# Channel shuffle: tiles of 51 KB a partition in two load and two store buffers, for tiles of 38 KB in two and three

## The chip, the cores and the metric

The kernel runs on one core of a Trainium2 chip. Its time is the device time of one launch in microseconds (us); it was measured in three runs. One further execution was taken with the hardware profiler, and the profile and the trace below are of that one.

A core has several engines with queues of their own. Three matter here: VectorE (DVE in the profile), which does the copies; SyncE (SP), whose queue issues the loads; and ScalarE (ACT), whose queue issues the stores. The bytes themselves are moved by 16 transfer (DMA) engines. Data sits in the main memory of the chip (DRAM) and is worked on in a buffer memory of 128 partitions.

## The reference

The input `x` is 16 x 64 x 64 x 256 in float32, 67.1 MB, and `groups` is 8. Every run of 256 channels is read as 8 groups of 32 and written as 32 x 8, a small transpose:

```python
x = x.reshape(batch, h, w, groups, channels_per_group)
x = x.transpose(0, 1, 2, 4, 3)
x = x.reshape(batch, h, w, c)
```

Nothing is computed with the values. 67.1 MB are read and 67.1 MB are written.

## The kernel before

The 65,536 pixels of 256 channels are 1 KB each. A tile with `q` in the list of slots takes 128 x `q` pixels that follow one another, and each of the 128 partitions gets `q` of them, so `q` KB that are contiguous in DRAM. A transfer of a tile so has 128 rows of `q` KB. "A tile of 38" below is one with 38 KB a partition, 4.98 MB in all.

The list `_SLOTS` (line 12) gives the tiles in order. An entry is a slot: it has one load buffer and one store buffer, and its parts share these. The first slot has two parts, of 4 and 8 KB; then come a slot of 28, twelve of 38 and one of 16, which adds up to 512 KB a partition.

For each slot the loop (lines 45 to 63) takes the next buffer of `in_pool` and of `out_pool`, issues the loads of all its parts on SP's queue (line 55), and then for each part a copy on VectorE (line 57) and a store on ACT's queue (line 61). The copy reads the source in steps of 32 elements (group, then channel in the group) and writes a contiguous run. As built, its source is walked in three levels, rows x 32 x 8, and its destination as a single run of 256 x rows elements.

The order of each queue is that of the code (`manual_schedule`). What else orders the work are the buffers, which are used in turn:

- A load waits until the copy that reads its buffer is done. With two load buffers that is the copy two slots back.
- A copy waits for its load, and until the stores that read its store buffer have landed. With three store buffers those are the stores three slots back, with two those of two slots back.
- A store waits for its copy.

The buffers are as large as the biggest slot: 2 x 38 + 3 x 38 = 190 KB a partition.

Of the kernel before, what the change touches and what calls it, by code (L numbers as in the profile page):

```python
# [1 line left out]

# [4 lines left out]


F32 = mybir.dt.float32
P = 128  # L10

_SLOTS = [[4, 8], [28]] + [[38]] * 12 + [[16]]
_IN_BUFS = 2
_OUT_BUFS = 3


@with_exitstack
def kernel(
    ctx: ExitStack,
    tc: tile.TileContext,  # L20
    x: bass.AP,
    groups: bass.AP,
    out: bass.AP,
):
    nc = tc.nc
    b, h, w, c = x.shape
    G = int(groups)
    CPG = c // G
    assert G * CPG == c
    assert sum(map(sum, _SLOTS)) * P == b * h * w  # L30
    biggest = max(map(sum, _SLOTS))

    x_flat = x.rearrange("b h w c -> (b h w c)")
    out_flat = out.rearrange("b h w c -> (b h w c)")

    in_pool = ctx.enter_context(tc.tile_pool(name="in_pool", bufs=_IN_BUFS))
    out_pool = ctx.enter_context(tc.tile_pool(name="out_pool", bufs=_OUT_BUFS))

    def rows(flat, first, q):

        return flat[first * c : (first + P * q) * c].rearrange("(p f) -> p f", p=P)

    ctx.enter_context(tc.manual_schedule(engines=None))
    first = 0
    for parts in _SLOTS:
        in_tile = in_pool.tile([P, biggest * c], F32, name="in_tile")
        out_tile = out_pool.tile([P, biggest * c], F32, name="out_tile")
        at = 0
        pieces = []
        for q in parts:  # L50
            pieces.append((q, first, slice(at * c, (at + q) * c)))
            first += P * q
            at += q
        for q, start, cols in pieces:
            nc.sync.dma_start(out=in_tile[:, cols], in_=rows(x_flat, start, q))  # L55
        for q, start, cols in pieces:
            nc.vector.tensor_copy(  # L57
                out=out_tile[:, cols].rearrange("p (i j g) -> p i j g", j=CPG, g=G),
                in_=in_tile[:, cols].rearrange("p (i g j) -> p i j g", g=G, j=CPG),
            )  # L60
            nc.scalar.dma_start(
                out=rows(out_flat, start, q), in_=out_tile[:, cols]
            )


# [1 line left out]
_INS = ['x', 'groups']  # L67
_OUTS = [((16, 64, 64, 256), 'float32')]

_NUMBERS = {'groups': 8}  # L70


# [26 lines left out]
```

## Time and profile before

| | us |
|---|---|
| median of the three runs (316.06 to 316.10) | 316.07 |
| span of the profiled execution | 314.4 |
| VectorE busy, 16 copies | 119.0 |
| one copy of 38 KB (128 x 9728 elements), mean of 12 | 8.79 |
| load of 38 KB, median from issue to landing | 37.0 |
| store of 38 KB, median from issue to landing | 42.6 |
| start of the first copy | 4.06 |
| start of the last copy (the slot of 16) | 294.54 |

The span is the stretch from the first to the last instruction of the profiled execution. The profile says for each engine how long it was busy, and for each instruction what ended the idle time ahead of it. Transfers are listed with the time from the issuing instruction to the landing of the last byte; that time contains the wait behind earlier transfers of the same queue. Over the whole span the transfer engines moved 427 GB/s in the mean.

### The profile page before, as it was taken

The numbers are of one execution on the slowest core, as the hardware profiler recorded it, in microseconds if no ns is written. First come the engines' busy times: TensorE is split into PE (matmuls) and PEld (weight loads), VectorE is DVE, ScalarE is ACT, GpSimd is POOL, SyncE is SP. The second block draws the span as 40 slices with busy tenths as digits, with TensorE's granted clock in tenths as the row PEclk, the third lists the DMA queues.
The fourth block names the chain that finished last, engine by engine and source line by source line (L and its number), as shares of the span: only waits on it lengthen the run. The fifth ranks groups of instructions, "written<-read, shape, count | busy, mean of one in ns | idle before, by whom it ended". The sixth has DMA issues, their size and how long they took to land.

```text
span 314.4 us, 132 instructions
## 1 busy us (share of the span) xinstructions
DVE 119.0 (38%) x16; POOL 0.2 (0%) x4
## 2 busy tenths in 40 slices
DVE  2081907309109109019028028037046055065400
POOL 0000000000000000000000000000000000000000
DMA  7999999999999999999999999999999999999997
GB/s 317 405 441 416 435 416 483 401 465 406 450 421 446 426 436 436 401 470 396 475 396 475 396 470 401 470 401 470 401 450 421 446 426 436 436 417 450 429 421 321
DMA packets 4608, 134.22 MB, mean 427 GB/s; under 512 B 512, under 2 KB 512, under 8 KB 768
## 3 DMA queue, kind: packets, MB, share of 16 engines
q1 hardware_dynamic: 2304, 67.11, 49.8%
q10 hardware_dynamic: 2304, 67.11, 49.4%
HBM read 67.11 MB, written 67.11 MB: 427 GB/s over the span
## 4 chain that ended last, share of the span: by engine, by line
DMA 76%; DVE 19%; issue 0%; SPq 0%; DVEq 0%
DMA in_tile<-in_x_dram 76%; DVE out_tile L57 19%; SPq L55 0%; DVEq L57 0%
## 5 line engine op out<-in xcount | busy, mean ns | idle before, releaser
L57 DVE COPY out_tile<-in_tile 128x9728 f32<-128x9728 f32 (+4 forms) x16 | 119.0, 7440 | 179.4 <-DMA in_tile<-in_x_dram 179.4
L80 POOL MEMSET const-uint8-127<- 128x1 uint8 x1 | 0.1, 103 | 0.0
L80 POOL MEMSET const-bfloat16-1.0<- 128x1 bf16 x1 | 0.1, 102 | 0.0
L80 POOL MEMSET const-float32-1.0<- 128x1 f32 x1 | 0.1, 100 | 0.0
L80 POOL MEMSET const-float32-0.0<- 128x1 f32 x1 | 0.1, 99 | 0.2 <-issue 0.2
## 6 DMA issues: line engine op xcount, KB each, us to landing
in_tile<-in_x_dram SPq DMA_DIRECT2D x12, 4864.0 KB, 37.0
out_dram<-out_tile ACTq DMA_DIRECT2D x12, 4864.0 KB, 42.6
in_tile<-in_x_dram SPq DMA_DIRECT2D x1, 3584.0 KB, 14.7
out_dram<-out_tile ACTq DMA_DIRECT2D x1, 3584.0 KB, 30.9
in_tile<-in_x_dram SPq DMA_DIRECT2D x1, 2048.0 KB, 30.4
out_dram<-out_tile ACTq DMA_DIRECT2D x1, 2048.0 KB, 15.2
in_tile<-in_x_dram SPq DMA_DIRECT2D x1, 1024.0 KB, 5.4
out_dram<-out_tile ACTq DMA_DIRECT2D x1, 1024.0 KB, 25.0
```

What stands on the lines that cost most here:

```text
L57: nc.vector.tensor_copy(out=out_tile[:, cols].rearrange("p (i j g) -> p i j g", j=CPG, g=G), in_=in_tile[:, cols].rearrange("p (i g j) -> ...
L80: nc = _bacc.Bacc("TRN2", target_bir_lowering=False, num_devices=1)
```

## The change

```diff
-_SLOTS = [[4, 8], [28]] + [[38]] * 12 + [[16]]
+_SLOTS = [[4, 4], [28]] + [[51]] * 9 + [[17]]
 _IN_BUFS = 2
-_OUT_BUFS = 3
+_OUT_BUFS = 2
```

The sum over the slots stays 512 KB a partition. The first slot has parts of 4 and 4, the second stays, twelve tiles of 38 become nine of 51, and the last has 17 for 16. There are 13 loads, 13 copies and 13 stores for 16 of each. The buffers take 4 x 51 = 204 KB a partition. The code of the loop is the same.

## The prediction

> **What bounds the kernel now.** I read the page's totals first, then the copies in order of time, then the waits, then the transfers by size.
>
> ```profile
> span 314.4 us, 132 instructions
> DVE 119.0 (38%) x16; POOL 0.2 (0%) x4
> ...
> q1 hardware_dynamic: 2304, 67.11, 49.8%
> q10 hardware_dynamic: 2304, 67.11, 49.4%
> ```
>
> VectorE works for 38% of the span. The load queue (q1) and the store queue (q10) together hold the 16 transfer engines for 99.2% of it. So the end is set by bytes: a change can win almost nothing, and loses whatever time the transfer engines stand still.
>
> ```profile
> 94.33 8.77 DVE L57 COPY out_tile<-in_tile 128x9728 f32<-128x9728 f32 x1 [14.27 <-DMA in_tile<-in_x_dram]
> 117.35 8.76 DVE L57 COPY out_tile<-in_tile 128x9728 f32<-128x9728 f32 x1 [14.25 <-DMA in_tile<-in_x_dram]
> ```
>
> The copies of 38 KB start 23.02 us apart. In that time one load and one store of 4.98 MB each go by: 9.96 MB / 23.02 = 432.8 GB/s, 27.05 GB/s for each transfer engine. One row (38 KB of one partition) therefore holds an engine for 1.44 us; by the same rate 51 KB takes 1.93, 28 KB 1.06, 4 KB 0.15. In brackets stands what each copy waited for:
>
> ```profile
> DVE out_tile L57 <- DMA in_tile<-in_x_dram: 179.4, 16, 14.3
> ...
> SPq L55 <- DVE out_tile L57: 106.2, 13, 8.9
> ```
>
> All 16 copies wait for their load, none for a store: the third store buffer is always free in time. In SP's queue 13 of 16 loads wait for the copy that empties their buffer.
>
> ```profile
> out_dram<-out_tile ACTq DMA_DIRECT2D x1, 1024.0 KB, 25.0
> ...
> in_tile<-in_x_dram SPq DMA_DIRECT2D x1, 512.0 KB, 3.3
> out_dram<-out_tile ACTq DMA_DIRECT2D x1, 512.0 KB, 14.3
> ```
>
> The small first stores land late. The 512 KB store is issued at 5.2 and lands at 19.5, the 1 MB store is issued at 8.6 and lands at 33.7. The 14.2 us between them are eight turns in which a 38 KB load row passes for each 8 KB store row: 8 x (1.44 + 0.31) = 14.0. So the queues alternate row by row, and a small store pays for the big load rows beside it.
>
> ```profile
> L57 DVE COPY out_tile<-in_tile 128x9728 f32<-128x9728 f32 x12 | 105.5, 8791 | 158.5 <-DMA in_tile<-in_x_dram 158.5
> L57 DVE COPY out_tile<-in_tile 128x7168 f32<-128x7168 f32 x1 | 6.6, 6569 | 7.7 <-DMA in_tile<-in_x_dram 7.7
> L57 DVE COPY out_tile<-in_tile 128x4096 f32<-128x4096 f32 x1 | 3.9, 3873 | 7.6 <-DMA in_tile<-in_x_dram 7.6
> L57 DVE COPY out_tile<-in_tile 128x2048 f32<-128x2048 f32 x1 | 2.0, 2019 | 1.5 <-DMA in_tile<-in_x_dram 1.5
> L57 DVE COPY out_tile<-in_tile 128x1024 f32<-128x1024 f32 x1 | 1.1, 1092 | 4.1 <-DMA in_tile<-in_x_dram 4.1
> ```
>
> From 7168 to 9728 elements the copy grows by 2222 ns: 0.868 ns an element, over a fixed part of 8791 - 9728 x 0.868 = 347 ns.
>
> **The change, part by part.**
>
> *Fewer, longer transfers.* The bytes stay. Each way there are 13 transfers for 16, so an engine moves 208 rows for 256. The trace's records of single rows give 0.159 us for 4 KB and 1.439 for 38 KB: 0.0084 us a row on top of the bytes. 48 rows fewer save 0.4 us. Bounds: 0 and 0.6. I take -0.4. The issue instructions (about 0.33 to 0.43 us each on SP and ACT, three fewer on each) lie under transfers and count nothing.
>
> *The copies of 51 and 17.* At the rate of the rows above a copy of 51 takes 347 + 13056 x 0.868 = 11.7 us, one of 17 about 4.1. But no row is of their kind. Every copy of before has an even number of 1 KB rows (4, 8, 16, 28, 38); 51 and 17 are odd. The source of a copy is walked as rows x 32 x 8, the destination as one run; for 38 rows half the run (4864) ends on a row, for 51 half the run (6528) is 25.5 rows. If VectorE works on two halves side by side, it can't here, and one stream pays each element twice: 347 + 13056 x 2 x 0.868 = 23.0 us, and 17 rows take about 8.0. Bounds: 11.7, and 23.6 if the whole 8791 scales and doubles. These ends are far apart, the parity is the one property in which all five rows known differ from the new ones, and I take 23.0.
>
> [...]
>
> *Two store buffers.* The first copy of 51 now waits for both 4 KB stores, where the third buffer spared it this. Behind it on VectorE stand all later copies, on ACT its store, on SP the third load of 51, which needs its input buffer. The 28 KB load starts 1.2 us sooner (0.52 MB less ahead), but the later turns of the first 4 KB store now pass 51 KB rows, so it lands at about 21, not 19.5; the second lands 8 x (1.93 + 0.15) = 16.7 later, at 38. The copy starts at 38.4 (0.4 from landing to copy, as in the rows of before) and ends at 61.4; its store and the third load of 51 move their first row about 1.0 later (the 512 KB load lands 3.3 us after its issue, of which its bytes take 1.2; I put half of the rest ahead): 62.4.
>
> What covers this? Until then the transfer engines have only loads of 4 + 4 + 28 + 51 + 51 = 138 KB and stores of 4 + 4 + 28 = 36 KB a partition: 174 KB, 22.8 MB, 52.7 us at 432.8 GB/s. From the first row at 1.7, and with 0.6 for the uneven start, they run dry at 55.0. First gap: 62.4 - 55.0 = **7.4 us**. With copies of 11.7 the first one ends at 50.1 and there is no gap; the cover is gone above 55.0 - 38.4 - 1.0 = 15.6 us.
>
> *The steady part.* After the gap the third load and the first store of 51 start together and share the engines: 13.37 MB, 30.9 us a tile. A buffer's round is copy 23.0 + 1.4 of lags + 30.9 = 55.3, and with two buffers it may take 2 x 30.9 = 61.8. Slack 6.5: no loss, the copy lies under the transfers of its neighbours.
>
> *The end.* Loads and stores go in step, so when the last load of 51 lands, the store two tiles back has landed too. What is left while its copy runs: the store before it and the load of 17: 51 + 17 KB, 8.91 MB, 20.6 us. The copy needs 0.4 + 23.0 + 1.0 = 24.4. Second gap: **3.8 us**; the copy of 17 (8.0) then lies under the last store of 51 (15.4). Before, the last copies took 8.7 and 3.9 with more than that still moving.
>
> *Sum*, on the profiled span: 314.4 - 0.4 + 7.4 + 3.8 = 325.2. The median of the runs, 316.07, lies 1.7 above the span (what is outside it, which nothing here alters): **326.9 us**.
>
> **Rivals.**
>
> *The copies keep the even rate (not slower).* For it: nothing in the trace shows a parity effect, and the five shapes lie within 13% of one line (347 + 0.868 an element). Against: they share the property that is lost. Then copies wait for stores: at the first 51 for 7 us (38, against its load's landing at 31), later for up to 8 x (1.93 - 1.06) = 7 more, since the rows of the 28 KB store pass load rows of 51. But 14 + 11.7 + 1.4 = 27.1 stays under 30.9, and no queue runs dry: 316.07 - 0.4 = 315.7. It decides below 15.6 us a copy; even the dearest rate of the rows (1.066 ns, the copy of 1024) gives 13.9.
>
> *The rounds of two buffers become the bound.* Its place is VectorE and the buffers together; its price: at twice the dearest rate a copy takes 27.8, the gaps 12.2 and 8.6 us: 336.5. Above 61.8 - 32.3 = 29.5 us every tile would lose as well. Against: the dear rate belongs to a copy so short that its fixed part weighs.
>
> *Two store buffers alone cost, with fast copies.* If the wait for a store exceeded 30.9 - 11.7 - 1.4 = 17.8 us, each further microsecond would count in nine tiles: at 19, 9 x 1.2 - 0.4 = 10.4, 326.5. Against: the lag of 14 above is an upper bound, and two queues that share evenly keep their lag.
>
> **How the numbers follow.** Forecast 0.79; even rate 0.15; rounds as the bound 0.04; the wait alone 0.02. A measurement of this kernel tells 0.2%, 0.6 us, from no change. The even rate gives -0.1%, so it splits: 0.10 same, 0.05 faster; the rest, 0.85, is slower. Range of the likeliest: at the low end the first gap alone, since a remainder of an earlier store hides the second, with the small store a turn sooner: 314.0 + 5.5 + 1.7 = 321.2; at the high end copies of 23.6 and the small store a turn (1.93) later: gaps of 9.9 and 4.4, 330.0. The other cases each lie far off; 321 to 330.5 leaves them out and holds some 8 in 10.
>
> **What would show it.** In the profile after: copies of 128x13056 at about 23,000 ns (VectorE near 224 us in all: 9 x 23.0 + 8.0 + 6.6 + 2.2); the first of them waiting for a store until about 38; transfer share low in two places only, near 55 to 62 and for 4 us some 25 us before the end; starts of copies 30.9 us apart between. Copies near 11,700 ns would make the forecast wrong at one blow, and the time 315.7. Copies at 23 without a first gap would mean that small stores land sooner than by turns.

## The result, and the profile after

The changed kernel takes 368.11 us (median of five runs, 367.13 to 369.52), the kernel before 316.07 in the same session. The ratio is 1.164, with a 95% interval from 1.163 to 1.166. The forecast was 326.9 with a range up to 330.5: slower was right, but four fifths of the loss were not foreseen.

The page of the changed kernel begins like this:

```profile
span 365.3 us, 115 instructions
...
DVE 217.2 (59%) x13; POOL 0.2 (0%) x4
...
q1 hardware_dynamic: 1872, 67.11, 48.6%
q10 hardware_dynamic: 1872, 67.11, 46.9%
...
out_dram<-out_tile ACTq DMA_DIRECT2D x2, 512.0 KB, 26.1
```

VectorE is busy for 217 us instead of 119, but that is still only 59%. The two transfer queues hold the engines for 95.5% of a span that is 51 us longer. So the transfer engines did not stand still for 51 us: they were occupied and moved less.

The groups of copies, shape by shape (busy time, mean ns of one, idle time before and what ended it):

```profile
L57 DVE COPY out_tile<-in_tile 128x13056 f32<-128x13056 f32 x9 | 200.9, 22344 | 119.1 <-DMA out_dram<-out_tile 119.1
L57 DVE COPY out_tile<-in_tile 128x4352 f32<-128x4352 f32 x1 | 7.6, 7642 | 0.0
L57 DVE COPY out_tile<-in_tile 128x7168 f32<-128x7168 f32 x1 | 6.6, 6615 | 9.4 <-DMA in_tile<-in_x_dram 9.4
```

The odd shapes take 1.71 and 1.76 ns an element, where the even shape of 7168 still takes 0.92. The copies of 51 wait for stores now (eight of the nine; the second follows the first at once), none for its load.

The same copies in order of time, with the issues at the first gap (SPq is the load's, ACTq the store's):

```profile
40.79 44.58 DVE L57 COPY out_tile<-in_tile 128x13056 f32<-128x13056 f32 x2 [18.41 <-DMA out_dram<-out_tile]
63.16 0.33 SPq L55 DMA_DIRECT2D in_tile<-in_x_dram  x1
63.17 0.36 ACTq L61 DMA_DIRECT2D out_dram<-out_tile  x1
...
175.69 22.34 DVE L57 COPY out_tile<-in_tile 128x13056 f32<-128x13056 f32 x1 [13.79 <-DMA out_dram<-out_tile]
211.66 22.34 DVE L57 COPY out_tile<-in_tile 128x13056 f32<-128x13056 f32 x1 [13.63 <-DMA out_dram<-out_tile]
```

The first copy of 51 starts at 40.8 and ends at 63.1; only then are the third load of 51 and the first store of 51 issued, both at 63.2. Later copies start 36.0 us apart, not 30.9, and VectorE is idle for 13.6 us of it. By stretches (length, VectorE busy, GpSimd busy, clock, share of the transfer engines, GB/s):

```profile
55.00:63.00 8.00, 8.00 (x2) 0.00 (x0) 1.00 0.13 57
63.00:103.00 40.00, 22.40 (x3) 0.00 (x0) 1.00 1.01 368
103.00:211.00 108.00, 66.98 (x3) 0.00 (x0) 1.00 0.99 368
211.00:284.00 73.00, 44.66 (x2) 0.00 (x0) 1.00 0.99 367
```

The first gap is there, at the place that was forecast. From its end on the engines are occupied without a pause, at 368 GB/s instead of 433. The trace's records of single rows show the same: a row of 51 KB takes 1.93 us in the median up to the gap, and after it a tile's rows take 2.2 to 2.4 us in the mean as long as both queues are full.

An account in bytes: between the two gaps 102.5 MB move (134.2 less 22.8 before the first and 8.9 after the second). At 432.8 GB/s that is 236.8 us. By the row records the stretch lasts from 64.1 to 341.5, 277.4 us. These 40.6 us account for the miss of the span (365.3 for 325.2); the other parts of the forecast nearly cancel.

### The profile page after: what moved, and what is told of

Same layout as the page of the kernel before. It is cut to its first block, busy times and chain, and to the rows that moved or that the text cites. A ratio compares the mean times of both kernels' runs of the same rounds, so it can differ in the third digit from the quotient of the medians.

```text
span 365.3 us, 115 instructions
## 1 busy us (share of the span) xinstructions
DVE 217.2 (59%) x13; POOL 0.2 (0%) x4
## 4 chain that ended last, share of the span: by engine, by line
DMA 49%; DVE 37%; another core or an unknown queue 8%; DVEq 2%; issue 0%; SPq 0%
DMA out_dram<-out_tile 48%; DVE out_tile L57 37%; DVEq L94 2%; DMA in_tile<-in_x_dram 1%; SPq L55 0%; DVEq L57 0%
## 5 line engine op out<-in xcount | busy, mean ns | idle before, releaser
L57 DVE COPY out_tile<-in_tile 128x13056 f32<-128x13056 f32 (+3 forms) x13 | 217.2, 16735 | 132.7 <-DMA out_dram<-out_tile 119.1
```

The lines of the kernel that those rows point to most:

```text
L57: nc.vector.tensor_copy(out=out_tile[:, cols].rearrange("p (i j g) -> p i j g", j=CPG, g=G), in_=in_tile[:, cols].rearrange("p (i g j) -> ...
```

## The experiments

Three theories stood at the start. Theory 1: a load and a store that start together after a dry queue (one that has no transfer left to do) move the same row of their tiles at the same time from then on ("in step"), and slow each other. Theory 2: long rows of some 51 KB in both queues are slow by themselves. Theory 3: copies of an odd row count slow the transfers beside them.

**Even tiles of 50**

```diff
-_SLOTS = [[4, 4], [28]] + [[51]] * 9 + [[17]]
+_SLOTS = [[4, 4], [28]] + [[50]] * 9 + [[26]]
```

> Nine tiles of 50 KB and one of 26 for nine of 51 and one of 17; four buffers as in the changed kernel. Theory 1 (the odd copies open a gap in the transfers; loads and stores then start together, run in step and slow each other): copies of 50 near 11,500 ns, no gap, 433 GB/s, about 315.7 us. Theory 2 (rows of some 51 KB in both queues at once are slow, whatever the copies do): copies near 11,500 ns but the rate between 60 and 300 us stays near 370 GB/s, and the time is over 350 us.

Four executions took 318.6, 318.7, 350.7 and 352.4 us. The profiled one, with a span of 316.9 us, has copies of 11.4 to 11.8 us, no gap ahead of the first large store and 427 to 435 GB/s from 50 to 290 us. So large rows can run at full rate, but the tiling does not do so each time. Neither theory had said that. No trace of a long execution of these tiles was kept.

**The copies alone undone**

```diff
-            nc.vector.tensor_copy(out=..., in_=...)
+            src, dst = ...
+            even = q - q % 2
+            nc.vector.tensor_copy(out=dst[:, :even], in_=src[:, :even])
+            if even < q:
+                nc.vector.tensor_copy(out=dst[:, even:], in_=src[:, even:])
```

> The changed kernel with each copy of 51 as one of 50 rows and one of 1, and that of 17 as 16 and 1; every transfer as in the changed kernel. Theory 1: 11,500 + some 400 ns a tile, no gap, about 315.7 us. Theory 2: the transfers are those of the changed kernel, so rows of 51 KB still take 2.2 us and more, and the time is over 350 us.

Its times were 319.7, 351.1, 355.2 and 358.6 us. The profiled execution has a span of 318.0, and every transfer of the changed kernel, but moves this:

```profile
150.00:200.00 50.00, 23.55 (x4) 0.00 (x0) 1.00 1.01 433
200.00:250.00 50.00, 14.43 (x3) 0.00 (x0) 1.00 1.00 435
```

Rows of 51 KB in both queues at 433 to 435 GB/s: theory 2, as stated, falls. The stretches before it hold 428 to 441 GB/s from 50 us on. What differs between two executions of one program was looked for in a further one:

> The kernel with the copies split into 50 rows and 1, once more, for a profile of one of its long executions (its four times were 319.7, 351.1, 355.2 and 358.6 us). Theory 1: in a long execution loads and stores of 51 KB begin within a row of each other and their rows take over 2.1 us; in a short one the load queue is a row or more ahead and rows take 1.93.

```profile
50.00:90.00 40.00, 14.24 (x4) 0.00 (x0) 1.00 1.01 433
90.00:120.00 30.00, 11.84 (x2) 0.00 (x0) 1.00 1.01 433
...
150.00:200.00 50.00, 11.68 (x2) 0.00 (x0) 1.00 1.01 409
200.00:250.00 50.00, 23.63 (x4) 0.00 (x0) 1.00 0.97 365
```

This execution took 355.9 us. It runs at full rate for 120 us, and from 200 us on at 365 GB/s until its loads are done. The records of rows and landings tell when: up to 170 us the load queue is a row or more ahead, in the mean (the sixth load of 51 starts at 148.6, the fourth store at 152.5). One of the 16 transfer engines falls behind meanwhile: of the third load of 51 fifteen engines land their share at 85.0 to 85.5 us and one at 92.2, of the fifth fifteen at 146.6 to 147.1 and one at 165.2. Copies wait for that one, so loads are issued late. At 177.6 the next load is issued just as the other engines run out of the one before (177.4 to 177.9), together with a store; they begin 2.5 us apart (a row of each takes 3.9), and load rows take 2.39 us in the mean. That is theory 1's pattern, reached by another road. Why one engine fell behind is not known.

**Two store buffers alone**

```diff
-_OUT_BUFS = 3
+_OUT_BUFS = 2
```
(in the kernel before, tiles of 38)

> The kernel before with two store buffers for three, tiles as they were. Both theories: copies wait for stores, but at 8.8 us a copy no queue runs dry: 316.1 us, within 0.3. A cost of the missing buffer by itself would show as a time over 317.

316.09 us, ratio 0.9999 (0.9985 to 1.0014). The waits of this kernel:

```profile
DVE out_tile L57 <- DMA out_dram<-out_tile: 167.8, 13, 14.3
```

Thirteen copies wait for a store, 167.8 us in all, and no loss shows (0.14% at most, by the interval). Here the wait of an engine that is not the bound costs nothing.

**Odd tiles of 41 with three store buffers** (against the changed kernel)

```diff
-_SLOTS = [[4, 4], [28]] + [[51]] * 9 + [[17]]
+_SLOTS = [[4, 4], [28]] + [[41]] * 11 + [[25]]
 _IN_BUFS = 2
-_OUT_BUFS = 2
+_OUT_BUFS = 3
```

> Eleven tiles of 41 KB and one of 25, all odd, with three store buffers (205 KB). Copies near 18.0 us. Theory 1: no gap ahead of the first large store, loads and stores stay out of step, 433 GB/s, 316 to 317 us. Theory 3 (a copy of an odd row count slows the transfers beside it by itself): a rate near 370 GB/s while copies run, over 340 us.

355.67 us, ratio 1.125 (1.123 to 1.127). The copies took 17.95 us as expected; the time was 39 us over what theory 1 had been made to say.

```profile
20.00:50.00 30.00, 21.80 (x3) 0.00 (x0) 1.00 1.01 432
50.00:90.00 40.00, 26.81 (x2) 0.00 (x0) 1.00 1.00 390
...
200.00:250.00 50.00, 31.39 (x2) 0.00 (x0) 1.00 0.98 376
```

The rate falls at 50 us. There was no gap, but the load queue alone ran dry: its second tile of 41 had its last row at 47.8, and the copy that frees the next buffer ended at 48.1. That load and the first store of 41 were issued together at 48.1 and began at 49.9 and 51.9. The expectation had asked only whether all transfers stop; a dry load queue is enough to get into step. Alone, this run could not tell theory 1 from theory 3. The next one does.

**The same odd tiles with three load buffers**

```diff
-_IN_BUFS = 2
-_OUT_BUFS = 3
+_IN_BUFS = 3
+_OUT_BUFS = 2
```

> The odd tiles of 41 KB again (copies near 18.0 us), now with three load and two store buffers, so that the load queue always holds its next load when one lands, and no load starts together with a store after a dry queue. Theory 1 (only being in step slows the transfers; odd copies by themselves cost nothing here): about 433 GB/s throughout, 316 to 319 us, against 355.7 with two load and three store buffers. Theory 3 (odd copies slow the transfers beside them): 340 us or more.

320.0 us, ratio 1.012 (1.010 to 1.014).

```profile
50.00:90.00 40.00, 29.23 (x3) 0.00 (x0) 1.00 1.00 433
...
200.00:250.00 50.00, 35.86 (x3) 0.00 (x0) 1.00 1.02 440
```

The same tiles, the same copies of 17.9 us, the same memory, and 425 to 444 GB/s in the stretches from 50 to 290 us: theory 3 falls. The 4 us over the kernel before lie near the end, where the last copy of 41 isn't covered (268 and 336 GB/s in the two slices of its page between 288 and 304 us); the expectation had missed that by a microsecond.

**Getting into step by one late copy, with even tiles of 38** (against the kernel before)

```diff
-_OUT_BUFS = 3
+_OUT_BUFS = 2
...
+            for _ in range(3 if start == P * 40 else 1):
+                nc.vector.tensor_copy(
```

> The kernel before with two store buffers, and the first copy of 38 done three times (26.4 us for 8.8), so that the transfers run dry once, near 50 to 61 us, and the third load of 38 and its first store start together. All other copies stay at 8.8 us. Theory 1 (loads and stores that move the same row of their tiles at the same time slow each other): the rate stays near 370 GB/s to the end and the time is about 360 us. Theory 2 (only rows of some 51 KB are slow) and theory 3 (only odd copies slow the transfers): the gap alone is paid, 11.7 us, 328 us.

339.31 us, ratio 1.073 (1.071 to 1.075): between the two.

```profile
20.00:50.00 30.00, 19.20 (x3) 0.00 (x0) 1.00 1.00 427
...
150.00:200.00 50.00, 17.60 (x2) 0.00 (x0) 1.00 1.00 412
```

After the gap (50.6 to 61.1 us by the row records) the rate stays at 411 to 418 GB/s as long as both queues are full, with even copies, short enough to hide, and the rows of before: store rows take 1.58 us instead of 1.44, and copies start 24.1 us apart instead of 23.0. So one late copy put a kernel that runs at 433 GB/s into a slower pattern that it did not leave. The effect is there at 38 KB, but a third as large as theory 1 had been made to say.

**Getting out of step with the changed kernel's own copies**

```diff
+    late_pool = ctx.enter_context(tc.tile_pool(name="late_pool", bufs=1))
...
+            if start == P * 36:
+                scratch = late_pool.tile([P, 512], F32, name="scratch")
+                for _ in range(8):
+                    nc.scalar.copy(out=scratch[:, :], in_=out_tile[:, :512])
             nc.scalar.dma_start(
```

> The changed kernel, with the first store of 51 held back by eight small ScalarE copies of its buffer (about 5 us in all), so that its load queue is two to three rows ahead of the store queue from then on. Theory 1: 433 GB/s after the first gap, about 327 us (the forecast of the record, the delay itself lying under loads). Theory 2 and 3: no change, 365 us or more.

357.87 us, ratio 1.131 (1.127 to 1.135). The total missed, the stretches decide (a column for ScalarE stands third here):

```profile
70.00:124.00 54.00, 35.57 (x2) 0.00 (x0) 0.00 (x0) 1.00 1.00 425
...
128.00:300.00 172.00, 111.37 (x5) 0.00 (x0) 0.00 (x0) 1.00 0.99 369
```

In one execution of one program, with the same copies of 22.3 us and the same rows: 425 GB/s while the load queue is two to four rows ahead, 369 after that. The change comes at 126.2, where the load queue has been empty since 124.4 (the landing of the load before) and a load and a store are issued together. The late store had made the next copy late: by this reading, the forecast's 6.5 us of slack were not enough for a lead and a long copy.

**Where do they collide?** First the addresses in DRAM:

```diff
+        n, at = divmod(first - P * 36, P * 51)
+        if q == 51 and 0 <= n < 9:
+            part = P * (36 + 51 * (n - n % 3))
+            whole = flat[part * c : (part + 3 * P * q) * c]
+            return whole.rearrange("(p k f) -> k p f", p=P, k=3)[n % 3]
```

> The changed kernel, with the nine tiles of 51 taken in groups of three whose rows interleave in DRAM: a partition reads 51 KB of every 153 KB. Copies, transfers, row sizes, waits and the step of loads and stores stay. Only the distance between the row that is loaded and the row that is stored at the same time changes: from a multiple of 256 KB to 102 KB or -51 KB over such a multiple. Theory 1a (the same rows collide in the memory because their addresses differ by such a multiple): 433 GB/s after the first gap, about 327 us. Theory 1b (being in step is enough, whatever the addresses): 365 us or more.

365.71 us, and between the gaps still:

```profile
103.00:211.00 108.00, 66.82 (x3) 0.00 (x0) 1.00 0.98 366
```

The control, with groups of two:

> The same with groups of two for the first eight tiles of 51: a partition reads 51 KB of every 102 KB, but tiles two apart still lie a multiple of 256 KB apart row by row. It is the control for the pitch. Theory 1a and 1b: as the changed kernel, 365 us or more. A time near 327 us here as well would say that the pitch of the rows decides and not the distance between load and store.

368.52 us and 369 GB/s. Neither these distances in DRAM nor the pitch of the rows mattered: theory 1a, as stated, falls, and 1b stands.

Then the rows that stand side by side. Loads and stores of 51 were each issued in two transfers:

```diff
+            for part in [slice(0, c), slice(c, q * c)] if q == 51 else [cols]:
+                nc.sync.dma_start(out=in_tile[:, part], in_=...)
...
+            for part in [slice(0, c), slice(c, q * c)][::-1] if q == 51 else [cols]:
+                nc.scalar.dma_start(out=..., in_=out_tile[:, part])
```

> The changed kernel, with each load of 51 issued as one of 1 KB and one of 50 KB a partition, and each store as one of 50 and one of 1: when a load and a store start together, the long rows of one partition no longer stand side by side, short rows of the other queue do. Copies, gaps and bytes stay. Theory 1 (the long load row and the long store row of the same partition, one after the other on an engine, hinder each other): rows of 50 KB at 1.89 us, 433 GB/s between the gaps, 327 to 331 us (the forecast of the record and some 2 us for 18 more transfers each way). If starting together is harmful in another way: over 360 us.

331.13 us, ratio 1.048 (1.047 to 1.050), a tenth of a microsecond over what theory 1 said (nine more transfers each way, 18 in all):

```profile
54.00:63.00 9.00, 9.00 (x2) 0.00 (x0) 1.00 0.47 193
63.00:300.00 237.00, 169.22 (x8) 0.00 (x0) 1.00 1.00 428
300.00:329.00 29.00, 13.71 (x2) 0.00 (x0) 1.00 0.72 309
```

Two gaps where the forecast has them (no row moves for 4.1 and for 6.2 us), and nearly the full rate between them, with all nine copies of 22.3 us. By the row records the stores' long rows stand beside 1 KB rows only for the first three or four rows of a tile. After that long rows of both queues alternate here too, but the store's are three to four rows ahead of the load's, and each takes 1.89 to 1.91 us in the mean. In the control the store's halves are issued in the load's order (the `[::-1]` is dropped):

> The control: the same numbers and sizes of transfers, but the store too issues its 1 KB first, so that long rows of the same partition stand side by side when both start together. Theory 1: slow as the changed kernel, 360 to 372 us. If the number or the sizes of the transfers made the difference in the run before: the same time as that run.

366.34 us, and between the gaps:

```profile
103.00:211.00 108.00, 65.75 (x4) 0.00 (x0) 1.00 0.99 371
```

The same transfers in the same number, only their order within a tile differs: 35 us. In the control the long rows are in step and take 2.1 to 2.2 us in the mean. So it is neither long rows side by side nor a common start as such, but the same row. This pair is the plainest evidence for theory 1.

The row records of the other runs sort the same way. Take the rows by which the load queue leads the store two tiles back, in the mean over the starts of store rows. Where the rate is full the lead is 1.3 to 4.7 rows: 2.2 in the kernel before, 2.7 with even tiles of 50, 1.5 in the shorter execution with split copies, 1.3 in the longer one up to 170 us, 4.7 with odd tiles of 41 and three load buffers, 3.2 after the late store up to 122 us. Where it is low the lead is half a row: 0.5 in the changed kernel, with odd tiles of 41 and three store buffers, with the late copy and in the control above, and 0.5 and 0.6 in the late-store run and the split copies after their fall.

Last, three runs and a fourth to find the place of the collision. Other partitions side by side, and the control:

```diff
+            for p in [slice(0, 16), slice(16, P)] if q == 51 else [slice(0, P)]:
+                nc.sync.dma_start(out=in_tile[p, cols], in_=rows(x_flat, start, q)[p])
...
+            for p in [slice(0, 112), slice(112, P)] if q == 51 else [slice(0, P)]:
+                nc.scalar.dma_start(out=rows(out_flat, start, q)[p], in_=out_tile[p, cols])
```

> The changed kernel, with each load of 51 issued as partitions 0 to 15 and then 16 to 127, and each store as 0 to 111 and then 112 to 127: a load and a store that start together stay a row or more apart in partitions. Long rows stand side by side as before. Theory 1p (the collision is at the same partition): about 430 GB/s between the gaps, 326 to 333 us. Theory 1r (any two long rows side by side collide when both queues start together): 355 us or more.

> The control: loads and stores both as partitions 0 to 15 and then 16 to 127, so the same partitions stand side by side. Theory 1p and 1r: 355 us or more. If transfers of 112 and 16 partitions were the reason of a difference: the same time as the run before.

431.5 to 440.7 us and 409.9 to 439.6: both far slower than the changed kernel, so they tell nothing of partitions. Tiles moved as 112 and 16 partitions are slow without any step: in the control the rows of the first load of 51 took 3.6 us in the mean, with hardly anything but 4 KB rows of the store queue beside them.

Rows of half the length, with the store's halves in the other order and then in the same order (the split above at `26 * c` instead of `c`):

> The changed kernel, with each load of 51 issued as the first 26 KB of every partition and then the other 25, and each store the other way round: the same partitions stand side by side, but other columns of them. Theory 1p: still slow, over 345 us. If the collision is between the same bytes of the tiles, or between rows of 51 KB alone: 326 to 333 us.

> The changed kernel, with each load and each store of 51 issued as the first 26 KB of every partition and then the other 25: when both start together, the same columns of the same partition stand side by side, in rows of half the length. If the length of the rows decides: as the run with the halves in opposite order, 330 to 341 us. If the same columns side by side decide: 355 us or more.

331.8 to 338.8 us and 330.2 to 335.4. From 63 to 300 us their profiled executions, of 338.3 and 335.4, move 420 and 426 GB/s:

```profile
63.00:300.00 237.00, 162.25 (x8) 0.00 (x0) 1.00 1.00 420
63.00:300.00 237.00, 167.02 (x8) 0.00 (x0) 1.00 1.00 426
```

The shortest executions of the two lie 1.5 us apart, so the order of the halves makes no difference of note. By the row records both runs are in step from 80 to 260 us, and rows of 25 and 26 KB hinder each other only a little. So the length of the rows is part of it. Whether the collision sits at the partition of the buffer memory, in a transfer engine or in DRAM stays open: the run that should have put other partitions side by side was slow from its shape alone.

No run beat the kernel before. It holds the engines for 99.2% of the span, and even the shortest of the other tilings, an execution of the even tiles of 50, took 318.6.

## Why the prediction was right and wrong

- *Fewer transfers, -0.4 us*: too small to be seen in any run here.
- *The copies*: 22.34 us and 7.64, where 23.0 and 8.0 had been taken and 11.7 was the other end. The choice by parity was right. The two odd shapes give 1.689 ns an element over a fixed part of 0.29 us, where 1.736 and 0.35 had been taken. The factor of two was the author's estimate: no run shows that VectorE works on two halves of a copy side by side. What the runs show is 1.71 to 1.76 ns an element at 51, 41, 25 and 17 rows and 0.89 to 0.92 at 50 and 28: 22.34 us for 51 rows, 11.4 to 11.8 for 50.
- *Two store buffers and the first gap*: the first copy of 51 started at 40.8 for 38.4, the transfers were dry at 57.4 for 55.0 (the last row's end by the records), and moved again at 64.1 for 62.4. A gap of 6.7 us for 7.4: right. So was its cause: the two small stores moved their last rows until 20.7 and 37.4 us, where landings at 21 and 38 had been forecast.
- *The steady part*: this is the step that failed. "After the gap the third load and the first store of 51 start together and share the engines: 13.37 MB, 30.9 us a tile." They did start together and did share the engines, but at 368 GB/s, 36.0 us a tile. The 432.8 GB/s came from a stretch of the kernel before in which the load queue is one to three rows ahead of the store queue, and was carried into a stretch where the two run in step. Nothing in the profile of before shows that pattern. So the term that was mis-sized is the transfer time of a tile. The slack of the copies (a round of 55.3 in 61.8) was sound: VectorE waited 13.6 us a tile.
- *The end*: the second gap was 1.8 us for 3.8 (341.5 to 343.3), presumably since the slower transfers covered more of the copy. The run with the 1 KB rows apart has both gaps and 428 GB/s between them, and takes 331.1 us. That is 4.2 over the forecast of 326.9, and its second gap of 6.2 us is part of it: this one term holds most of the miss, not quite all.
- *The rivals*: the even rate for odd copies did not occur. The loop of two buffers as the bound is excluded by the idle 13.6 us a tile; that two store buffers alone cost nothing is shown with tiles of 38 (316.09 us, ratio 0.9999). What happened, transfers that slow each other, was in no rival; the prediction held the rate of the engines for a constant.
- Among the signs named ahead were copies "30.9 us apart between" the gaps. That sign came out at 36.0 and pointed to the failed step at once.

## What to carry to other kernels

A copy of this kernel with an odd row count cost about twice as much as one with a row less (22.3 us at 51 rows, 11.4 to 11.8 at 50, 11.7 to 11.9 for 50 rows and then 1); split off the odd row or choose even tiles. In a kernel that is bound by transfers, watch whether the load queue runs dry: the first stall itself cost 7 us here, but restarting both queues together cost 40. Where long rows of loads and stores must run side by side, shorter rows, or a lead of one queue of a row or more, are worth a try (here 420 to 428 GB/s instead of 368), and a rate that was measured in one pattern of the queues is a rate of that pattern.

## What the runs showed of the hardware

- Two queues that were both full moved about 433 GB/s with the load queue a row or more ahead, and 428 with the store queue three to four rows ahead. In step, with a lead of less than a row, they moved 368 GB/s with rows of 51 KB, 371 with 50 and 1, 376 to 392 with 41, 411 to 418 with 38, and 420 to 426 with 25 and 26. These runs differ in other things too; only the pair with 50 and 1 (428 and 371) differs in nothing but the order of its stores.
- The step was kept while both queues were full: after one late copy, 411 to 418 GB/s from 90 to 290 us. With rows of 51 KB one execution also slid into it at 178 us, and executions of that program took 319.7 to 358.6 us. The tiles of 50 spread likewise (318.6 to 352.4), but no trace shows why.
- A tile moved as 16 and 112 partitions was slower than as 128: the rows of its first load of 51 KB took 3.6 us in the mean instead of 1.93.
